# Reordering loads and statistics in a block of two half-step FFNs and a two-part mixer on eight cores

## The chip, the cores and the metric

One Trainium2 chip, eight cores, each working through two of the sixteen sequences. The two dies have cores 0 to 3 and 4 to 7. The metric is the device time of the slowest core, in microseconds. In slow executions a die's mean granted clock is lower; only fast ones are compared.

## The reference, cut

```python
D_MODEL, BATCH, SEQ, D_FF, EPS = 1024, 16, 2048, 2816, 1e-6

def rms_norm(x, g):
    y = x * lax.rsqrt(jnp.mean(x * x, axis=-1, keepdims=True) + EPS)
    return y * g

def swiglu(h, w_gate, w_up, w_down):
    return (jax.nn.silu(h @ w_gate) * (h @ w_up)) @ w_down

# one layer (cut):
x = x + 0.5 * swiglu(rms_norm(x, ffn1_norm), ffn1_w_gate, ffn1_w_up, ffn1_w_down)
h = rms_norm(x, mix_norm)
# ... h @ w_in gives q, k, v of a forgetting attention (8 heads x 64, causal, decay bias)
# ... and q, k, v, gates of a gated linear attention (4 heads, chunks of 64 frames)
x = x + concat(fox, gla) @ w_out
x = x + 0.5 * swiglu(rms_norm(x, ffn2_norm), ffn2_w_gate, ffn2_w_up, ffn2_w_down)
# and a final rms_norm
```

## The kernel before

A core has 4096 tokens, in eight groups of 512. The first FFN of groups 0 and 1 runs as a pair, so that the weights, which come as 32-bit numbers, are used twice in the stretch where the DMA engines are full (busy share 0.98 to 1.05 from 40 to 100 us, core 6); from then on a group's mixer runs interleaved with other groups' FFNs. The program is written as a list of operations with what they read and write. A scheduler in the program simulates the engines with estimated durations and so fixes the order on each engine; `level` is an operation's rank (0 is highest).

```python
        # DMA's end in the scheduler's simulation:
                dma_free = max(dma_free, t + o.dur) + o.nbytes / (o.rate * 1000.0)
                o.end = dma_free + 2000.0 + o.slack
```

A weight tile's first use loads it with a cast by the POOL queue and stores the bf16 copy; later uses load that copy by the SP queue. Some tiles are cast ahead in the background.

```python
        def LOADW(tag, wb, tile, src, keep, i, reads=()):
            # ...
            if key in uses:
                DMA("sp", (tag, wb, "b"), tile, keep[i], 2 * n, reads=[key], writes=[(tag, wb)])
                return
            uses.add(key)
            DMA("pool", (tag, wb), tile, src[i], 4 * n, reads=reads, writes=[(tag, wb)], slack=3000.0)
            DMA("sp", (tag, wb, "s"), keep[i], tile, 2 * n, reads=[(tag, wb)], writes=[key], level=1, slack=3000.0)
```

A norm's squares are summed over the 1024 channels with a matmul against ones; four small operations make the reciprocal root of it, and then the row of 512 values must be spread over the 128 partitions. There are two ways: eight small matmuls (0.61 us in the timeline of core 1) and an ACT copy (`spread`), or out to memory and back with a broadcast (`send`), which costs PE two such matmuls but takes two DMAs.

```python
        def rsqrt_columns(who, n, scale, bank, level):
            v, pw, hl = stat[who]
            TS(v[:, 0:n], banks[bank][:, 0:n], scale, EPS, ALU.mult, ALU.add, [], [PS(bank), ("stv", who)], level=level)
            P.op("pool", ...pow..., level=level)
            CP(hl[:, 0, 0:n], pw[:, 0:n], [("stp", who)], [("sth", who)], level=level)
            TT(hl[:, 1, 0:n], pw[:, 0:n], hl[:, 0, 0:n], ALU.subtract, [("stp", who)], [("sth", who)], level=level)

        def send_columns(who, n, out, otags, bank, level):
            # ... 2 matmuls and an ACT copy to stg
            DMA("sp", ("rw", who), rows_d[i, ...], stg[0:n, :], ..., writes=[("row", i)], level=level, slack=600.0)
            DMA("sp", ("rr", who), out, rows_d[i:i + 1, ...].broadcast_to([128, n * 128]), n * 65536,
                reads=[("row", i)], writes=otags, level=level, slack=800.0)
```

The start: x of group 0 on three queues, then weights, and the pair's first three tiles for each group.

```python
        for k in range(8):
            DMA(("sp", "act", "pool")[k % 3], ("x0", k), x_sb[:, 0, k, :], x_d[0, ...], 128 * 2048, writes=[("x", 0, k)], rate=0.35)
        DMA("sp", "gains", gT[:], gains_d[:, :], 16384, writes=["gT"])
        # ...
                todo = [(c, L) for c in range(NC2) for L in lanes]
                if pair and half == 0:
                    todo = [(c, L) for L in lanes for c in range(3)] + todo[6:]
```

The softmax here doesn't subtract the row's maximum and nothing guards it: scores larger than these inputs give would overflow.

Of the kernel before, what the change touches and what calls it, by code (L numbers as in the profile page):

```python
# [239 lines left out]
def build_nc():  # L240
# [17 lines left out]
    with contextlib.ExitStack() as st:  # L258
# [146 lines left out]
        for w in ("F", "M"):  # L405
# [3 lines left out]
                                               fill=1.0, base=0, channel_multiplier=1), [], ["ident", "setup"], dur=400)  # L409
        for k in range(8):  # L410
            DMA(("sp", "act", "pool")[k % 3], ("x0", k), x_sb[:, 0, k, :], x_d[0, k // 2, :, (k % 2) * T:(k % 2 + 1) * T], 128 * 2048,
                writes=[("x", 0, k)], rate=0.35)
        DMA("sp", "gains", gT[:], gains_d[:, :], 16384, writes=["gT"])
# [22 lines left out]
        DMA("sp", "c_fb", fb[:], fb_d[:, :], 32, writes=["fb"])  # L436
        DMA("sp", "c_gon", gon[:], gon_d[:, :], 512, writes=["gon"])
        TSS(gon[:], gon[:], 0.5, ALU.mult, [], ["gon"])
        DMA("pool", "c_wg2a", wg2a[96:113, :], wg2a_d[:, :], 17 * 1024, reads=["wg2a"], writes=["wg2a"])
        DMA("pool", "c_wmisc", wmisc[:].rearrange("p k c -> p (k c)"), wmisc_d[:, :], 163840, writes=["wmisc"])  # L440
# [8 lines left out]
        def LOADW(tag, wb, tile, src, keep, i, reads=()):  # L449
# [3 lines left out]
            if key in uses:  # L453
                DMA("sp", (tag, wb, "b"), tile, keep[i], 2 * n, reads=[key], writes=[(tag, wb)])
                return
# [4 lines left out]
        def background(gate):  # L460
            if tiles:
                src, keep, i = tiles.pop(0)
                uses.add((keep.tensor.name, i))
                DMA("pool", ("cast", len(tiles)), keep[i], src[i], 4 * 128 * keep.shape[2], reads=[gate],
                    writes=[(keep.tensor.name, i)], slack=6000.0)
# [5 lines left out]
        def rsqrt_columns(who, n, scale, bank, level):  # L471
            v, pw, hl = stat[who]
            TS(v[:, 0:n], banks[bank][:, 0:n], scale, EPS, ALU.mult, ALU.add, [], [PS(bank), ("stv", who)], level=level)
            P.op("pool", lambda e: e.tensor_tensor(out=pw[:, 0:n], in0=v[:, 0:n], in1=mhalf[:, 0:n], op=ALU.pow),  # L474
                 [("stv", who), "mhalf"], [("stp", who)], dur=390.0 + 141.0 * n, lat=250.0, level=level)
            CP(hl[:, 0, 0:n], pw[:, 0:n], [("stp", who)], [("sth", who)], level=level)
            TT(hl[:, 1, 0:n], pw[:, 0:n], hl[:, 0, 0:n], ALU.subtract, [("stp", who)], [("sth", who)], level=level)
# [19 lines left out]
        class Norm:  # L497
# [20 lines left out]
            def sums(self, bank):  # L518
# [6 lines left out]
                rsqrt_columns(self.who, 4, 1.0, bank, level)  # L525
# [39 lines left out]

        def norm_later(norm, then):
            def spread(gate):
                norm.send(nxt("fb", 3))
                then()
# [4 lines left out]
        class Raw:  # L574
# [7 lines left out]
            def emit(self):  # L582
                for k in range(8):
                    TS(self.h[:, k, :], x_sb[:, self.g, k, :], gT[:, k:k + 1], 1.0, ALU.mult, ALU.mult, [("x", self.g, k), "gT"],
                       [(self.tag, k)], level=0.1)
                    self.norm.add(k, 6 + self.g)
                self.norm.finish(6 + self.g)
                TT(self.square, self.rstd, self.rstd, ALU.mult, [self.rtag], [self.qtag], level=0.1)

        def ffn(f, lanes, middle, nextx=None, casts=(0, 0), second=None, ending=None, late=False):  # L590
            pair = len(lanes) == 2
            xtiles = (5, 7, 9, 10) if late else (3, 5, 7, 9)
            for half in range(2):
                todo = [(c, L) for c in range(NC2) for L in lanes]
                if pair and half == 0:
                    todo = [(c, L) for L in lanes for c in range(3)] + todo[6:]
                where = {}
                for n, (cl, L) in enumerate(todo):
                    if second is not None and half == 0 and n == 2:
                        second()  # L600
                    if cl not in where:
                        where[cl] = wb = nxt("wgu", 4)
                        LOADW("wgu", wb, wgu[:, wb, :], wgu_d[f], wgu_s[f], half * NC2 + cl,
                              [("x", 0, 5)] if cnt["wgu"] <= 3 else [("x", 1, 7)] if cnt["wgu"] == 4 else ())
                    wb = where[cl]
                    w4 = wgu[:, wb, :].rearrange("p (g k f) -> p g k f", g=2, k=8)
                    bg = nxt("fb", 3)
                    bu = nxt("fb", 3)
                    raw = L.raw if half == 0 and cl < 3 else None
                    h, hk = (L.h, L.hk) if raw is None else (raw.h, raw.hk)  # L610
                    for g, b in ((0, bg), (1, bu)):
                        for k0, k1 in ([(k, k + 1) for k in range(8)] if cnt["wgu"] == 1 and g == 0 else [(0, 4), (4, 8)]):
                            MM(banks[b][:], [(w4[:, g, k, :], h[:, k, :]) for k in range(k0, k1)],
                               [("wgu", wb)] + hk[k0:k1], [PS(b)], start=k0 == 0, stop=k1 == 8)
                    r = nxt("th", 2)
                    if raw is None:
                        ACTV([(thF[:, r, :], banks[bg][:], AF.Tanh, None, 0.5)], [], [PS(bg), ("th", r)], level=0)
                    else:
                        TT(thF[:, r, :], banks[bg][:], raw.rstd, ALU.mult, [raw.rtag], [PS(bg), ("th", r)], level=0)
                        ACTV([(thF[:, r, :], thF[:, r, :], AF.Tanh, None, 0.5)], [], [("th", r)], level=0)  # L620
                        TT(banks[bu][:], banks[bu][:], raw.square, ALU.mult, [raw.qtag], [PS(bu)], level=0)
# [14 lines left out]
                for d in range(8):  # L636
                    wb = nxt("wd", 4)
                    LOADW("wd", wb, wd[:, wb, :], wd_d[f], wd_s[f], half * 8 + d, [("x", 1, 7)] if cnt["wd"] <= 4 else ())
                    for L in lanes:
                        b = ring[n % 2]  # L640
                        n += 1
                        for c0, c1 in ((0, 5), (5, NC2 - 1), (NC2 - 1, NC2)):
# [4 lines left out]
                            [PS(b), ("x", L.xb, d)], level=0)  # L647
# [18 lines left out]
        def ffn1_pair(middle):  # L666
# [4 lines left out]
            def second():  # L671
                for k in range(0, 8, 2):
                    load_x(1, k, ("wgu", 0))
# [23 lines left out]
        def last_down(L):  # L697
# [6 lines left out]
            for d in range(8):  # L704
                if d < 4:
                    wb = nxt("wd", 4)
                    LOADW("wd", wb, wd[:, wb, :], wd_d[1], wd_s[1], 8 + d)
# [445 lines left out]
```

## Time and profile before

| | before |
|---|---|
| time, median of 4 runs | 2671.16 us (2667.99 to 2679.67) |
| spans of the eight cores in the profiled run | 2652.0 to 2667.5 us, mean 2660.2 |
| PE busy | 96% |
| last of the 96 matmuls of the start | 52.1 us |

The profile's views are read in this order: the busy shares, PE's waits by what ended them, PE's timeline where the waits lie. The prediction shows their lines.

### The profile page before, as it was taken

The page shows a single profiled execution, that of the slowest core. Times are in us where ns is not written, and L with a number is a line of the kernel's source. Part 1 is how long each engine was busy: PE and PEld are TensorE (multiplying, and loading weights), DVE is VectorE, ACT ScalarE, POOL GpSimd, SP SyncE. Part 2 cuts the span into 40 slices and gives each one's busy share as a digit, 9 for nine tenths or more (in the row PEclk, how much of TensorE's full clock was granted, in tenths as well). Part 3 has the DMA queues.
Part 4 walks back from the last instruction along what each step waited for, and adds up shares of the span by engine and source line. Part 5 has one row for each costly group of instructions (what it writes and reads, how often), then busy time and mean ns, then how long its engine had stood idle before and what let it go on. Part 6 is the DMA issues. An engine that isn't in the chain of part 4 may idle for free.

```text
span 2667.5 us, 42806 instructions; the slowest of 8 cores (2652.0 to 2667.5 us)
## 1 busy us (share of the span) xinstructions
PE 2559.5 (96%) x13691; PEld 1173.9 (44%) x13940; DVE 1724.2 (65%) x2807; ACT 951.5 (36%) x2070; POOL 766.1 (29%) x768
## 2 busy tenths in 40 slices
PE   6999998989999999999999999999999999999998
PEld 3444453533543344533445344543445434533444
DVE  6334477658577845678756864569645697678754
ACT  2112223235326513166431411335222364266413
POOL 2213014124234512145421321024410254055410
PEclk9999999989999999999999999999999999999999
DMA  9987787595563355544455454553644433434353
GB/s 206 208 166 175 172 204 156 149 192 153 161 222 123 125 178 165 164 135 140 134 160 167 138 186 151 158 179 111 203 156 143 147 119 114 148 112 146 110 166 122
DMA packets 129866, 417.71 MB, mean 157 GB/s; under 512 B 15311, under 2 KB 17680, under 8 KB 129424
## 3 DMA queue, kind: packets, MB, share of 16 engines
q1 hardware_dynamic: 108128, 340.94, 40.2%
q0 software_dynamic: 20544, 72.98, 14.5%
q8 instruction: 117, 1.92, 0.3%
q10 hardware_dynamic: 976, 1.05, 0.1%
q14 instruction: 101, 0.83, 0.1%
HBM read 404.49 MB, written 59.86 MB: 174 GB/s over the span
## 4 chain that ended last, share of the span: by engine, by line
PE 84%; DVE 5%; issue 4%; DMA 4%; POOL 1%; ACT 1%; DVEq 0%; SPq 0%; POOLq 0%; ACTq 0%
PE bank L335 84%; DVE hF L379 1%; DMA rstdM<-rows 1%; DVE Pt L376 1%; DVE x_sb L379 1%; DMA mixw_t<-mixw 1%; DMA wd<-wds 1%; DMA wgu<-wgu 1%; ACT Pt L364 1%; POOL rstdM L376 1%; DMA rows<-wg2at 0%; DVE ga L376 0%; POOL ga L376 0%; DMA mixws<-mixw_t 0%; DMA gT<-gains 0%
## 5 line engine op out<-in xcount | busy, mean ns | idle before, releaser
L335 PE MATMUL bank<-hF,wgu 128*128 128x512 bf16 x5088 | 1181.4, 381 | 25.8 <-DVE thF L379 5.5
L335 PEld LDWEIGHTS bank<-hF,wgu 128*128 128x128 bf16 x5232 | 489.4, 98 | 628.6 <-issue 91.0
L335 PE MATMUL bank<-act,wd 128*128 128x512 bf16 (+2 forms) x2581 | 583.6, 376 | 16.3 <-DMA wd<-wds 8.1
L364 ACT ACTIVATE thF<-bank 128x512 f32<-128x512 f32 x346 | 207.3, 599 | 927.2 <-PE bank L335 924.0
L364 ACT ACTIVATE Pt<-bank,biasT 128x256 bf16<-128x256 f32 (+1 forms) x1152 | 428.5, 477 | 132.6 <-PE bank L335 127.8
L379 DVE SCALAR_TENSOR_TENSOR thF<-thF,bank 128x512 f32<-128x512 f32 x352 | 240.2, 682 | 256.1 <-ACT thF L364 248.6
L335 PEld LDWEIGHTS bank<-act,wd 128*128 128x128 bf16 x2640 | 247.9, 98 | 319.9 <-issue 44.5
L376 POOL TENSOR_TENSOR ga<-ga,Pt 128x512 f32<-128x512 f32 (+3 forms) x256 | 286.3, 1118 | 210.6 <-ACT Pt L364 118.9
L379 DVE SCALAR_TENSOR_TENSOR x_sb<-bank,x_sb 128x512 f32<-128x512 f32 (+2 forms) x264 | 175.9, 667 | 176.7 <-PE bank L335 174.3
L376 DVE TENSOR_TENSOR act<-bank,thF 128x512 bf16<-128x512 f32 x330 | 225.8, 684 | 65.4 <-PE bank L335 59.2
L376 DVE TENSOR_TENSOR ga<-ga,Pt 128x512 f32<-128x512 f32 (+3 forms) x256 | 206.4, 806 | 46.3 <-ACT Pt L364 36.7
L364 ACT ACTIVATE sqF<-x_sb 128x512 bf16<-128x512 f32 (+2 forms) x184 | 110.3, 609 | 265.8 <-DVE x_sb L379 219.0
L335 PE MATMUL bank<-hM,mixw_t 128*128 128x512 bf16 x875 | 197.8, 379 | 3.0 <-DVE cc L379 1.6
L335 PE MATMUL bank<-mixw_t,hM 128*128 128x256 bf16 x1280 | 143.1, 274 | 3.1 <-DMA mixw_t<-mixw 3.1
L335 PEld LDWEIGHTS bank<-mixw_t,hM 128*128 128x128 bf16 x1280 | 125.7, 98 | 20.8 <-issue 3.3
L376 POOL TENSOR_TENSOR rstdM<-rstdM,sqF 128x512 f32<-128x512 f32 x84 | 104.5, 1244 | 96.9 <-ACT sqF L364 85.8
L335 PEld LDWEIGHTS bank<-hM,mixw_t 128*128 128x128 bf16 x896 | 85.6, 98 | 104.6 <-issue 5.9
L474 POOL TENSOR_TENSOR stpM<-stvM,mhalf 128x8 f32<-128x8 f32 (+1 forms) x26 | 36.7, 1412 | 284.3 <-DVE stvM L383 284.3
L335 PE MATMUL bank<-cc,mixw_t 128*128 128x512 bf16 x500 | 116.9, 385 | 1.0 <-DVE x_sb L376 0.3
L335 PE MATMUL bank<-QT,KT 64*128 64x512 bf16 (+3 forms) x640 | 86.7, 349 | 12.6 <-DVE Pt L376 8.2
L1009 DVE RECIPROCAL sqM<-sqM 128x128 f32<-128x128 f32 x96 | 90.7, 945 | 11.6 <-ACT sqM L364 10.1
L335 PE MATMUL bank<-Pt,V 128*64 128x512 bf16 (+3 forms) x640 | 89.3, 359 | 0.8 <-DVE Pt L376 0.7
(162 smaller groups left out, 1987.4 us busy)
## 6 DMA issues: line engine op xcount, KB each, us to landing
wgu<-wgus SPq DMA_DIRECT2D x294, 512.0 KB, 3.7
wd<-wds SPq DMA_DIRECT2D x210, 352.0 KB, 3.2
mixw_t<-mixws SPq DMA_DIRECT2D x112, 512.0 KB, 3.8
wgu<-wgu POOLq DMA_DIRECT2D x36, 512.0 KB, 9.6
wgus<-wgu SPq DMA_DIRECT2D x36, 512.0 KB, 9.2
x_sb<-x POOLq DMA_DIRECT2D x28, 512.0 KB, 6.2
y<-x_sb POOLq DMA_DIRECT2D x56, 256.0 KB, 3.3
wd<-wd POOLq DMA_DIRECT2D x26, 352.0 KB, 6.4
```

Source lines behind the costliest of these rows:

```text
L335: ins = e.matmul(out, lhsT=l, rhs=r, start=s0, stop=s1)
L364: ins = e.activation(out=out, in_=in_, func=func, **kw)
L376: return DVE(lambda e: e.tensor_tensor(out=out, in0=a, in1=b, op=op), free_n(out), reads, writes, rate, eng, level)
L379: return DVE(lambda e: e.scalar_tensor_tensor(out=out, in0=a, scalar=s, in1=b, op0=op0, op1=op1), free_n(out), reads, writes, level=level)
L474: P.op("pool", lambda e: e.tensor_tensor(out=pw[:, 0:n], in0=v[:, 0:n], in1=mhalf[:, 0:n], op=ALU.pow), [("stv", who), "mhalf"], [("stp", ...
L1009: P.op("dve", lambda e, a=rcp[:, qs], b=src: e.reciprocal(out=a, in_=b), [], sq2 + ([PS(OB)] if p == 3 else []), dur=860.0, lat=180.0)
```

## The change

Its intent is to take PE's few long waits away without touching the arithmetic. Its four parts and their cost carry the prediction's letters: (a) a start in which the first three weight tiles are loaded beside x, into the idle buffers of the mixer, with group 1's x next and all else waiting, and 64 dummy matmuls, to have PE's clock up when the first weights come (it was 0.50 after the wait at 431 us, core 6 of the kernel before); (b) loads of gate/up and down tiles held back until the stage before is half done; (c) one norm spread by matmuls instead of rows, and four background casts moved from an FFN to the mixer of group 1; (d) the statistics' small operations at the highest rank, and the last mixer's squares summed by PE alone; (e) is what the holding costs. The diff, cut to its core:

```diff
+        DMA("sp", "gains", gT[:], gains_d[:, :], 16384, writes=["gT"], rate=0.25)
         for k in range(8):
-            DMA(("sp", "act", "pool")[k % 3], ("x0", k), ...)
+            DMA(("sp", "act")[k % 2], ("x0", k), ..., rate=0.25)
+        for i, cuts in enumerate(((0, 512, 1024, 2048), (0, 1024, 2048), (0, 1024, 2048))):
+            for j, (c0, c1) in enumerate(zip(cuts, cuts[1:])):
+                DMA("pool", ("first", i, j), mixw[:, i, c0:c1], wgu_d[0][i][:, c0:c1], 512 * (c1 - c0),
+                    reads=[("x", 0, 4)] if i == 1 else [("first", 0, 2)] if i == 2 else [], ...)
+        MMS([(banks[7][:, 0:128], onesD[:], onesD[:], True, True) for _ in range(64)], ["onesD"], [PS(7)])
+        for k in range(8):
+            DMA("sp", ("x1", k), x_sb[:, 1, k, :], ..., reads=[("first", 1, 1)], writes=[("x", 1, k)], rate=0.25)
 # ... first_tiles(): the 96 matmuls, group 0 k by k in its first tile, group 1 k by k over all three
                         LOADW("wgu", wb, ..., half * NC2 + cl,
-                              [("x", 0, 5)] if cnt["wgu"] <= 3 else [("x", 1, 7)] if cnt["wgu"] == 4 else ())
+                              [("x", 1, min(2 * cnt["wgu"] + 1, 7))] if cnt["wgu"] <= 4 else [("down", 2 * cl)] if cl < 4
+                              else ())
-                    LOADW("wd", wb, ..., half * 8 + d, [("x", 1, 7)] if cnt["wd"] <= 4 else ())
+                    LOADW("wd", wb, ..., half * 8 + d, [(lanes[-1].atag, 2 * d + 2)] if d < 4 and (pair or (wd_s[f].tensor.name, half * 8 + d) in uses) else ())
         def norm_later(norm, then):
+            later[0] += 1
+            here = later[0] == 2
             def spread(gate):
-                norm.send(nxt("fb", 3))
+                (norm.spread if here else norm.send)(nxt("fb", 3))
-            ffn(1, ..., middle, nextx, (0, 7 if tg == 0 else 0), ...)
+            ffn(1, ..., middle, nextx, (0, 0), ...)
 # in mixer(tgg), after the first QT, KT, V tiles and after kdec:
+                if tgg == 1 and i == 0:
+                    background(("QT", 1), -1)
 # in rsqrt_columns, four times:
-            ..., level=level)
+            ..., level=0)
-            norm = Norm(xb, sqM, "sqM", rstdF2[:, tgg % 2], ("rstdF2", tgg % 2), None)
+            norm = Norm(xb, sqM, "sqM", rstdF2[:, tgg % 2], ("rstdF2", tgg % 2), None, tgg == NTG - 1)
```

## The prediction

> **What bounds the kernel now.** I read the page's totals first, then the list of what TensorE (PE) waited for, then PE's timeline in the few stretches where the waits lie, and last the timelines of VectorE (DVE) and of the DMA issues there. All lines are of core 6, the slowest.
>
> ```profile
> PE 2559.5 (96%) x13691; PEld 1173.9 (44%) x13940; DVE 1724.2 (65%) x2807; ACT 951.5 (36%) x2070; POOL 766.1 (29%) x768
> ...
> PE 84%; DVE 5%; issue 4%; DMA 4%; POOL 1%; ACT 1%; DVEq 0%; SPq 0%; POOLq 0%; ACTq 0%
> ```
>
> PE is busy 2559.5 of 2667.5 us, so 108 us of idle time is all that a change of order can take back, apart from matmuls that run at a lowered clock. The change removes no matmul of the model. The list of PE's waits says where the idle time sits:
>
> ```profile
> PE bank L335 <- ACT sqF L364: 14.4, 6, 8.3
> PE bank L335 <- DVE thF L379: 11.3, 7, 4.4
> PE bank L335 <- DVE Pt L376: 9.0, 17, 1.9
> PE bank L335 <- DMA wd<-wds: 8.1, 1, 8.1
> PE bank L335 <- issue: 6.7, 42, 0.2
> PE bank L335 <- DVE sthF L376: 5.4, 2, 2.9
> PE bank L335 <- DMA wgu<-wgus: 4.6, 1, 4.6
> ```
>
> (total us, times, longest.) The big ones are single events, not a steady leak: one wait of 8.1 us for a down-projection tile, one of 4.6 us for a gate/up tile, one of 8.3 us for the first squares. So I go by stage. PE's timeline of the start (start us, us, what, idle before):
>
> ```profile
> 8.32 0.35 PE L335 MATMUL bank<-onesD,sqF 128*128 128x1 bf16 x8 [8.32 <-ACT sqF L364]
> ...
> 18.69 6.73 PE L335 MATMUL bank<-hM,wgu 128*128 128x512 bf16 x23
> 27.62 4.44 PE L335 MATMUL bank<-hM,wgu 128*128 128x512 bf16 x12 [2.21 <-DVE thF L379]
> ...
> 45.23 0.90 PE L335 MATMUL bank<-cc,wgu 128*128 128x512 bf16 x2 [3.43 <-DVE thF L379]
> 46.35 5.91 PE L335 MATMUL bank<-cc,wgu 128*128 128x512 bf16 x21 [0.22 <-DVE thF L379]
> 52.10 1.89 PE L335 MATMUL bank<-hF,wgu 128*128 128x512 bf16 x8
> ```
>
> The first matmul of the FFN is at 18.69 us. The three first weight tiles for both token groups (96 matmuls) are done at 52.10. Eight such matmuls take 1.89 us at full clock, some 20.8 us for 96, so 31 us are lost before 52.1. Two later stretches:
>
> ```profile
> 439.47 4.42 PE L335 MATMUL bank<-act,wd 128*128 128x512 bf16 x10 [8.13 <-DMA wd<-wds]
> ```
>
> ```profile
> 552.58 3.57 PE L335 MATMUL bank<-hF,wgu 128*128 128x512 bf16 x8 [4.60 <-DMA wgu<-wgus]
> 560.53 3.57 PE L335 MATMUL bank<-hF,wgu 128*128 128x512 bf16 x8 [4.38 <-DVE thF L379]
> 565.97 0.28 PE L335 MATMUL bank<-gq,Sbf 128*128 128x64 bf16 x4 [1.87 <-DVE Sbf L376]
> 567.93 0.37 PE L335 MATMUL bank<-gq,Sbf 128*128 128x64 bf16 x4 [1.69 <-DVE Sbf L376]
> ```
>
> ```profile
> 557.72 2.08 DVE L379 SCALAR_TENSOR_TENSOR hM<-x_sb,gT,rstdM 128x512 bf16<-128x512 f32 x3 [12.64 <-DMA rstdM<-rows]
> ```
>
> DVE stood 12.64 us before a product that needs rstdM, which came by a DMA out to memory and back; the thF product that PE needed was behind it.
>
> [...]after each gap above eight 128x512 matmuls take 3.57 us instead of 1.89. A gap thus costs its length and about 1.7 us more. [...]a DMA share of 1.04 in 20 to 30 us with two queues active. So moving the x tiles from three queues to two costs nothing. [...]in the trace the second alone, issued at 536.52, landed at 557.62: 21 us, of which most is queueing behind weights.
>
> **The change, part by part.**
>
> (a) The start. Gains go first. The first three weight tiles load at once into the mixer's idle buffers beside x0, the second group's x follows, and everything else (four down tiles, their stores, the stores of these three tiles) waits. 64 dummy matmuls warm the array. The order of instructions shows the gate matmuls now taken k by k as x arrives, before the statistics. What must arrive is unchanged: x0 2.10 MB, three tiles of 1.05 MB read, x1 2.10 MB, 7.34 MB in all. In the old trace x0, issued from 1.06 us, was in at 11.7; the weights were issued only then and landed at 17.7, 21.9 and 26.2, 4.2 us each or 0.25 MB/us. x0 and tile 0 together (3.15 MB) are then in at about 1.1 + 2.5 + 12.6 = 16 us, tile 1 at 20, tile 2 and x1 (another 3.15 MB, side by side) at 33. Tile 2 lies near 28, and group 1 needs eight k steps of six matmuls, 8 x 1.3 = 10.4 us, after that. With a partly cold clock [...]I put the end of the 96 matmuls at 43 us, against 52.1: 9 us. Against it stands DVE: three evacuations of four DVE operations of 0.68 us (8.2 us), eight hF2 products of 0.74 (5.9) and those of the next tiles (4.1) crowd into about 14 us, perhaps 2 us lost. The eight scalings of x1 move to ACT and spare DVE 8 x 0.48 = 3.8 us. The next tile's small DMA wait at 58 and similar ones: 1 us. Sum: 8 us.
>
> (b) Loads held back. A gate/up tile 0 to 3 of a half now waits for down tile 0, 2, 4, 6 of the half before, and a stored down tile d below 4 for activation tile 2d+2. In the trace the down tile awaited at 431 was issued at 422.2, behind three gate/up tiles of 1.05 MB issued at 406 to 415 for a stage that starts much later, and needed 17 us to land. With those behind it the wait goes: 8.1 us of idle and 4.42 - 2.2 = 2.2 us of cold clock. I count 8 of the 10.3.
>
> (c) The norm at 530. The second of these norms is spread by eight small matmuls (0.6 us) and an ACT copy (0.6) instead of the two DMAs, and four background casts move from the second FFN of group 0 to the mixer of group 1, where DMA has room (it ran at 0.4 to 0.5 in 480 to 520 us on another core). The stretch 547 to 570 loses 4.6 + 4.4 + 1.9 + 1.7 us of idle and twice 1.7 of cold clock: 16 us. I count 14.
>
> (d) Small things. The statistics' operations get the highest rank: 26 of them, PE waits of 1.3 us at 463 and the like: 1 us. In the last mixer PE sums the squares directly, without the POOL additions of 1.24 us: of the 2.8 us waited for hF at 2536 I count 2 us with the clock.
>
> (e) Cost. [...]There are 28 half passes of one group. I allow 2 us in all.
>
> Sum: 8 + 8 + 14 + 1 + 2 - 2 = 31 us; 2671 - 31 = 2640 us.
>
> **The rivals.** First, transfers hidden no better: the start is bound by the 7.34 MB, and x and weights side by side delay x, so that group 0 begins as late as before. For it: the DMA engines are at 0.9 to 1.0 for the first 100 us. Against: they sit idle after 11.7 us until the weights stream, and five tiles that nobody needs yet run in between. It would give 2648. Second, the wait moves: the held loads become late in every FFN, 28 times 1 us, or the DMA backlog of the start comes back at 100 to 300 us, where PE now waits for nothing. Against: a half's down part lasts 8 x 11 matmuls, 19 us, and a 512 KB load has a median of 3.7 us to landing. It would give 2660 to 2670. Third, DVE binds the start, group 1's three tiles being evacuated at once: 2645. Fourth, all goes well, the 3 us wait for mixer weights at 316 goes too and the cores draw together (they spread from 2652.0 to 2667.5, mostly by these same DMA waits): 2625.
>
> **Range and chances.** The parts are fairly independent; (a) may be 0 to 14, (b) 0 to 11, (c) 6 to 17, (e) up to 15. I predict 2640, with 2625 to 2657 for 8 in 10. Faster by over 2% means below 2617.7, a gain of 53 us; that is half of all idle time and beyond what the named stretches hold, 0.05. Slower by over 2%: 0.005. Within 2%: 0.945.
>
> **What would show it.** In the new profile: (a) the 96 matmuls end at 41 to 46 us, with the chain of waits there on DMA and not on the statistics; (b) no wait for wd at 400 to 440; (c) no DVE wait for rstdM near 500 to 550, and PE's clock there at 1.00; (d) the last hF wait under 2 us; (e) PE's waits for wgu and wd elsewhere under 3 us in sum. I am wrong if the start ends at 50 or later, if new DMA waits over 5 us stand between 100 and 400 us or after 600, or if the moved casts make the mixer of group 1 wait.

What is marked as cut in it are rules and figures that were not read from this case's traces. The sum came to 8 + 8 + 14 + 1 + 2 - 2 = 31 us, so 2640. Two of its numbers stand as estimates: the end of the 96 matmuls at 43 us, as far as it counts on a lowered clock in the k steps and on 2.5 us before x streams (in the trace x0 took 10.6 us; its 2.10 MB at the 0.25 MB/us of the weights leave 2.2), and the 2 us of (e). "Cold clock" is a granted clock of 0.50 in the windows of core 6 at 439 to 444, 552 to 556 and 560 to 564 us; it is 1.00 at 120 to 140. The two queues with a share of 1.04 are q0 and q1, at 0.78 and 0.26. The 34 transfers that bring a row back took 3.6 to 21.1 us on core 6, 4.3 at the median, so most of the 21 us is delay; the weight loads and stores issued beside it took 13.9 to 18.2 us to land, but that they are its cause was tested only later, by `e4_norm_by_rows`.

## More of the kernel before

One more view matters later: the span and the mean granted clock by die.

```profile
die 0 (median of its cores): 2659.1 us, clock 0.993
die 1 (median of its cores): 2662.3 us, clock 0.992
```

Both dies have practically the full clock (0.993 and 0.992).

## The result and the profile after

The changed kernel took 2657.38 us (median of 10 runs, 2654.29 to 2661.43) against 2670.46 of the kernel before beside it (median of 15, two of them slow). Ratios here are the mean time of one kernel's fast runs over that of the other's of the same rounds, so not quite the ratio of these medians: 0.9949, 95% interval 0.9939 to 0.9959. The gain is 13 us where 31 were predicted, and the time lies 0.4 us outside the predicted range.

The profile after is of core 5, the slowest. The page's totals and the chain that ended last:

```profile
PE 2590.9 (97%) x14034; PEld 1180.1 (44%) x14034; DVE 1717.5 (65%) x2797; ACT 956.6 (36%) x2079; POOL 762.7 (29%) x759
...
PE 85%; DVE 6%; DMA 4%; issue 3%; ACT 1%; POOL 0%; SPq 0%; DVEq 0%; ACTq 0%; POOLq 0%
```

PE's busy time is not to be compared with the 2559.5 us of before: there 13691 matmuls stand beside 13940 weight loads, so some 250 records are missing, and here none. In the chain the share of what has no visible reason (issue) fell from 4% to 3% and that of DVE rose from 5% to 6%; DMA stayed at 4%. The view by die is the first thing that stands out:

```profile
die 0 (median of its cores): 2639.3 us, clock 0.994
die 1 (median of its cores): 2652.2 us, clock 0.986
```

Die 0 gained 19.8 us over its median before, die 1 only 10.1. In all ten fast runs the slowest core was on die 1, and the mean clock of that die was below that of die 0. What PE waited for (total us, times, longest):

```profile
PE bank L335 <- DVE hF L379: 4.7, 1, 4.7
PE bank L335 <- DMA mixw_t<-wgu: 4.7, 1, 4.7
...
PE bank L335 <- DMA mixw_t<-mixw: 3.8, 3, 3.1
...
PE bank L335 <- DMA wd<-wds: 2.1, 2, 1.4
```

The waits of 8.1 us for a down tile, of 4.6 us for a gate/up tile and the 14.4 us for squares are gone from the list. New ones are the first weight piece (4.7 us, in the first 13 us) and the mixer's weights; the wait for hF at the end grew from 2.8 to 4.7 us. PE's timeline of the start (start us, us, what, idle before):

```profile
1.41 5.48 PE L335 MATMUL bank<-onesD 128*128 128x128 bf16 x64 [1.41 <-POOL onesD L394]
...
12.25 1.01 PE L335 MATMUL bank<-hM,mixw_t 128*128 128x512 bf16 x2 [4.68 <-DMA mixw_t<-wgu]
...
22.59 8.84 PE L335 MATMUL bank<-hM,mixw_t 128*128 128x512 bf16 x33
...
45.31 10.99 PE L335 MATMUL bank<-hF,wgu 128*128 128x512 bf16 x43
```

The dummies were 0.107 us apart until 4.7 us, 0.056 after that and 0.066 from 5.9; they were over by 6.9. PE then waited 4.68 us for weights, and the first real pair of matmuls took 1.01 us at a granted clock of 0.50 (12 to 14 us; 0.51 from 14 to 22). The 96 matmuls were done by 45.3 (42.7 on core 1), against 52.1. Look at the third line: 33 matmuls took 8.84 us, 0.268 each, at a clock of 0.81 (22 to 31 us); the 27 at 444 us in the next view, at 1.00, took 0.222 each. The stretch of the old wait for the down tile:

```profile
444.24 6.00 PE L335 MATMUL bank<-act,wd 128*128 128x512 bf16 x27
...
458.83 1.89 PE L335 MATMUL bank<-hM,wmisct 128*40 128x512 bf16 x8 [0.73 <-DVE x_sb L376]
461.66 0.37 PE L335 MATMUL bank<-wg2at,pieces 17*128 17x256 bf16 x2 [0.94 <-DVE pieces L391]
462.84 0.24 PE L335 MATMUL bank<-onesD,sqF 128*128 128x1 bf16 x4 [0.81 <-DVE sqF L391]
464.04 0.24 PE L335 MATMUL bank<-onesD,sqF 128*128 128x1 bf16 x4 [0.96 <-DVE sqF L376]
464.48 5.30 PE L335 MATMUL bank<-cc,mixw_t 128*128 128x512 bf16 x16 [0.20 <-DMA mixw_t<-mixw]
```

The down tiles no longer wait. But at the start of the mixer of group 1 five waits of under 1 us stand in a row, and the 16 matmuls after them take 5.30 us, at a mean clock of 0.68; in the kernel before (core 1) the same 16 took 3.63, at 1.00:

```profile
468.37 3.63 PE L335 MATMUL bank<-cc,mixw_t 128*128 128x512 bf16 x16
```

Short waits for DVE stood before these there too: 0.30, 1.34, 0.36 and 1.48 us on that core.

**Where the time went, by stage.** I laid each core's matmuls out by the work done before them (each at its full-clock time, 0.216 us for 128x512, the median distance of two at 120 to 140 us of the kernel before, core 6, at clock 1.00; dummies count nothing), so that the loss at a given work is how late PE was. The table has the change of the loss against the profiled run of before, mean of the eight cores, in us; the columns are the stages in us of PE work done. In every trace two of the eight cores lack some 250 matmul records, which shifts their stages; without these two cores single cells change by up to 2 us and sums by up to 4. The cores' mean span in the profiled run of before, 2660.2 us, was some 2 us above that of its fast runs on chips 3, 6 and 9 (2657.5 to 2658.6), so totals read about 2 us too good.

| kernel | 0-60 start | 60-350 | 350-410 down tile | 410-450 mixer 1 begins | 450-550 norm | 550-1000 | 1000-1300 | 1300-2480 | 2480 to the end, last mixer | sum |
|---|---|---|---|---|---|---|---|---|---|---|
| changed, first runs | -6.0 | +0.4 | -7.7 | +3.5 | -11.0 | +2.2 | +2.1 | -1.0 | +2.4 | -15.0 |
| changed, chips 3, 6, 9 (mean) | -8.6 | -0.2 | -7.8 | +4.1 | -10.3 | -0.8 | +2.0 | -2.7 | +0.8 | -23.4 |
| no hold | -8.3 | +1.8 | 0.0 | -0.1 | -10.6 | +3.9 | +0.8 | -1.4 | -0.3 | -14.1 |
| casts back | -8.4 | -0.5 | -8.2 | +5.0 | -4.7 | +3.3 | +2.6 | -3.6 | +0.9 | -13.5 |
| second norm by rows | -8.6 | +0.3 | -7.8 | +4.7 | -8.9 | -0.6 | +2.1 | -3.1 | +0.8 | -21.0 |
| old rank | -8.7 | +2.5 | -7.3 | +4.4 | -10.1 | +5.0 | +2.7 | -0.9 | +3.7 | -8.8 |
| last sums by POOL | -8.5 | -0.1 | -8.1 | +4.6 | -10.1 | -1.4 | +2.1 | -2.8 | +1.9 | -22.2 |
| start alone | -8.2 | +2.8 | -0.3 | +0.1 | 0.0 | -0.9 | -0.4 | -0.4 | -0.1 | -7.3 |
| norm and casts alone | -0.7 | -1.0 | -1.2 | +0.2 | -10.3 | +2.3 | +0.1 | -1.7 | 0.0 | -12.4 |
| rank alone | +0.1 | -1.3 | -1.0 | +0.1 | -0.8 | +6.3 | +0.1 | -0.2 | -0.2 | +3.0 |
| longer hold | -9.0 | -0.7 | -8.4 | +4.8 | -2.5 | +1.7 | +2.5 | -2.8 | +0.9 | -13.4 |
| rows later | -8.8 | +0.5 | -8.1 | +4.3 | -10.3 | +1.9 | +3.8 | +1.5 | +0.8 | -14.5 |
| old rank, rows later | -8.0 | +1.8 | -7.6 | +4.2 | -11.8 | +1.2 | +4.0 | +4.3 | +3.5 | -8.4 |

Three theories came out of this first profile. A: the terms were right and a lowered clock on one die of this chip took the rest. B: holding loads back moved the waits (the +3.5 at 410 to 450 and the mixer's weights). C: the small parts, rank and last sums, did harm.

### The profile page after: what moved, and what is told of

Its sections match the earlier page's. It is cut to its first block, busy times and chain, and to the rows that moved or that the text cites. A ratio compares the mean times of both kernels' runs of the same rounds, so it can differ in the third digit from the quotient of the medians.

```text
span 2659.8 us, 43278 instructions; the slowest of 8 cores (2634.5 to 2659.8 us)
## 1 busy us (share of the span) xinstructions
PE 2590.9 (97%) x14034; PEld 1180.1 (44%) x14034; DVE 1717.5 (65%) x2797; ACT 956.6 (36%) x2079; POOL 762.7 (29%) x759
## 4 chain that ended last, share of the span: by engine, by line
PE 85%; DVE 6%; DMA 4%; issue 3%; ACT 1%; POOL 0%; SPq 0%; DVEq 0%; ACTq 0%; POOLq 0%
PE bank L335 85%; DMA mixw_t<-mixw 2%; DVE hF L379 1%; DVE x_sb L379 1%; DMA wd<-wds 1%; DVE sqM L1060 1%; DVE Pt L376 1%; ACT Pt L364 1%; DMA ga<-rows 1%; DMA rstdM<-rows 1%; DVE act L376 1%; DMA x_sb<-x 0%; DVE hM L379 0%; DVE ga L376 0%; DMA mixws<-mixw_t 0%
## 5 line engine op out<-in xcount | busy, mean ns | idle before, releaser
L335 PE MATMUL bank<-hF,wgu 128*128 128x512 bf16 x5232 | 1194.0, 381 | 8.5 <-DVE hF L379 4.7
L335 PE MATMUL bank<-act,wd 128*128 128x512 bf16 (+2 forms) x2640 | 592.0, 378 | 4.8 <-DVE x_sb L379 2.5
L335 PE MATMUL bank<-hM,mixw_t 128*128 128x512 bf16 x944 | 216.3, 385 | 7.1 <-DMA mixw_t<-wgu 4.7
L335 PE MATMUL bank<-cc,mixw_t 128*128 128x512 bf16 x560 | 134.7, 394 | 0.9 <-DVE cc L376 0.6
L379 DVE SCALAR_TENSOR_TENSOR hF<-x_sb,gT,rstdF 128x512 bf16<-128x512 f32 x120 | 89.1, 789 | 2.8 <-ACT rstdF L364 2.0
```

What stands on the lines that cost most here:

```text
L335: ins = e.matmul(out, lhsT=l, rhs=r, start=s0, stop=s1)
L379: return DVE(lambda e: e.scalar_tensor_tensor(out=out, in0=a, scalar=s, in1=b, op0=op0, op1=op1), free_n(out), reads, writes, level=level)
```

## The experiments

All kernels below gave correct results. Where a table says "fast", it gives how many of the runs were fast and their mean.

### Does the gain depend on the chip? (the change unedited, three more times)

No edit.

> The changed kernel itself, unedited, as the control of these runs: the four kernels of the first call ran on another chip than the changed kernel's first runs. Theory C (the lowered clock of 0.812 belongs to the chip of the first runs, not to the dummies): on a chip whose die 1 shows no 0.812 stretches in fast runs it takes 2645 to 2650, as the kernel without the dummies did, and the spans of the two dies are alike. Theory W (the dummies set it off): die 1 is again 10 us longer than die 0 at a clock under 0.990, and the time is 2655 to 2660. If this chip shows the stretches for the other kernels of this call too, theory C stands as well.

> The changed kernel unedited, as the yardstick for these three and a third reading of the change: ratio 0.990 to 0.993 on a chip with clocks of 0.994 to 0.996 on both dies; 0.994 to 0.996 on a chip where one die is at 0.985 to 0.992, with stretches at 13/16 of the clock.

> The changed kernel unedited, a fourth reading, side by side with the next. If the chip lowers the clock of pairs of cores to 13/16, as the one of the first runs did, the ratio is 0.994 to 0.996 and the slowest core is on the die concerned; on a chip that doesn't, 0.990 to 0.993.

| run | chip | fast runs of all | mean | before, mean | ratio (95%) |
|---|---|---|---|---|---|
| after_again | 6 | 4 of 6 | 2647.8 | 2670.6 | 0.9916 (0.9901 to 0.9931) |
| g0_after_third | 9 | 3 of 7 | 2648.4 | 2670.3 | 0.9923 (0.9903 to 0.9943) |
| h0_after_fourth | 3 | 4 of 4 | 2648.6 | 2672.2 | 0.9910 (0.9895 to 0.9925) |

The dies of the first of these:

```profile
die 0 (median of its cores): 2638.3 us, clock 0.995
die 1 (median of its cores): 2635.2 us, clock 0.994
```

and on its core 5, the stretch of the start that took 8.84 us before, from the timeline:

```profile
22.36 7.29 PE L335 MATMUL bank<-hM,mixw_t 128*128 128x512 bf16 x33
```

On three other chips the change gains 22 to 24 us, not 13. The clock records of the first runs show what was different: on die 1 stretches at a granted clock of 0.8125 (the 0.812 and the 13/16 of the expectations), mostly of 15.1 us, always on a pair of cores (4 and 5, or 6 and 7) at the same moment: cores 4 and 5 at 21 to 54 us, and at 75, 250, 653, 770 and 1889; cores 6 and 7 at 29, 52, 645, 741, 765 and 2605 (the last for over 36 us). The first of all is at 5 us on cores 4 and 5, while the dummies ran. By an estimate from that clock, a busy stretch of 15.1 us costs 15.1 x (1 - 0.8125) = 2.8 us. The profile before has one such stretch on two cores (1892 us); the fast profiled runs on chips 2, 3, 6 and 9 have none. In the profiled run PE's busy time inside such stretches, times 0.1875, is 19 to 21 us on each core of die 1. The ten runs also carry their own control, the undisturbed die: the slowest core of die 0 was on average 11.2 us (5.1 to 14.8) ahead of the slowest of die 1, and with die 0 alone the mean time would have been 2645.9 us; on chips 3, 6 and 9 the slowest cores of the two dies are within 1.5 us on average. Theory A holds for some 10 of the missing 18 us. Two things stay open: only one batch of runs fell on that chip, so chip and moment can't be told apart; and why the kernel before, run beside it, kept its time there.

### Is it the dummy matmuls?

`e1_no_warmup`, the changed kernel without them (run again as `h1_no_warmup_again` next to the unedited one), and `e2_warmup_alone`, the kernel before with them:

```diff
-        MMS([(banks[7][:, 0:128], onesD[:], onesD[:], True, True) for _ in range(64)], ["onesD"], [PS(7)])
```

> The changed kernel without the 64 dummy matmuls; every engine's order is otherwise the same. Theory W (the dummies set off the lowered clock of 0.812 on die 1, which then costs the slowest core its gain): the 0.812 stretch at 5 us is gone, those of cores 4 to 7 in the first 80 us become fewer or go, cores 4 to 7 reach the spans of die 0, and the time falls to 2645 to 2652. Rival L ([...]the lowered clock comes anyway, dummies or not): 0.812 stretches on die 1 stay at 20 to 80 us and later, and the time stays within 2655 to 2660. On either theory the start itself loses nothing, because the changed kernel's array stood idle for 1 to 4.7 us after the dummies and ran its next matmuls at half clock: the 96 first matmuls end within 1 us of 42.7 (die 0).

> The kernel before with only the 64 dummy matmuls added at its start; order otherwise the same. Theory W: 0.812 stretches appear on die 1 in the first 80 us, where the kernel before had none, and the time rises by 3 to 8 us over the kernel before. Rival L: no such stretches at the start[...]; time within 2 us of the kernel before.

> The changed kernel without the 64 dummy matmuls, again. On a chip that lowers the clock: if the dummies bring it on, this kernel has no such stretch in the first 60 us and a ratio of 0.990 to 0.993, where the kernel with them has 0.994 to 0.996; if they don't, both are alike. On a chip that doesn't lower it, both are within 3 us, as they were on another chip.

| run | chip | fast | mean | ratio to before (95%) |
|---|---|---|---|---|
| e1_no_warmup | 6 | 4 of 6 | 2646.2 | 0.9906 (0.9891 to 0.9922) |
| h1_no_warmup_again | 3 | 4 of 4 | 2648.3 | 0.9909 (0.9892 to 0.9925) |
| e2_warmup_alone | 6 | 3 of 6 | 2671.0 | 1.0002 (0.9986 to 1.0017) |

The dummies are inert: beside the unedited kernel, without them, the time is the same (0.9906 against 0.9916, 0.9909 against 0.9910). The timeline of the kernel without them, core 1, shows why:

```profile
9.45 1.01 PE L335 MATMUL bank<-hM,mixw_t 128*128 128x512 bf16 x2 [1.20 <-DMA mixw_t<-wgu]
```

The pair takes 1.01 us there too: with the dummies the granted clock was at 0.50 again when the weights came (12 to 14 us, core 5 of the first runs). Whether they bring on the stretches at 0.8125 on a chip inclined to them is open: none of the later fast runs showed any, with dummies or without.

### What does holding the loads bring, and what does it cost?

`e3_no_hold` keeps the hold in the first FFN only:

```diff
-                              [("x", 1, min(2 * cnt["wgu"] + 1, 7))] if cnt["wgu"] <= 4 else [("down", 2 * cl)] if cl < 4
-                              else ())
+                              [("x", 1, min(2 * cnt["wgu"] + 1, 7))] if cnt["wgu"] <= 4 else ())
-                    ... if d < 4 and (pair or (wd_s[f].tensor.name, half * 8 + d) in uses) else ())
+                    ... if d < 4 and pair else ())
 # ... and the last FFN's down tiles likewise
```

> The changed kernel with the loads held back only in the first half of the pair; later gate/up and down tiles load as soon as their buffer is free, as before. If step (b) is right, the wait for a down tile near 410 to 440 us comes back with 5 to 10 us. If the hold is also what costs 4 us between 700 and 1300 us of work (theory H: bunched loads slow the row transfers of the norms from some 6 to 7 us to 9 us), those transfers are back at 6 to 7 us and the stretch loses 4 us less, so that the time is 0 to 5 us above the changed kernel. Rival R (the new rank of the statistics costs there): the row transfers and the loss of 700 to 1300 stay as in the changed kernel, and the time is 5 to 10 us longer.

Measured: 2654.9 (5 fast of 7, chip 6), ratio 0.9941 (0.9929 to 0.9954), so 7 us more than the unedited kernel on that chip. The wait for the down tile is back (PE's timeline, core 1):

```profile
435.32 3.93 PE L335 MATMUL bank<-act,wd 128*128 128x512 bf16 x10 [6.71 <-DMA wd<-wds]
```

In the table the row "no hold" has 0.0 at 350 to 410, and also -0.1 at 410 to 450. So the +4.1 there is the price of the hold, as theory B says: part of what is saved is paid back 20 us later. Core 5 of the unedited kernel shows the payment:

```profile
451.67 0.24 PE L335 MATMUL bank<-onesD,sqF 128*128 128x1 bf16 x4 [0.97 <-DVE sqF L376]
453.63 6.29 PE L335 MATMUL bank<-cc,mixw_t 128*128 128x512 bf16 x16 [1.73 <-DMA mixw_t<-mixw]
```

The mixer's tile was issued at 436.07 on core 1 and took 14.4 us to land, with gate/up tiles that were held until then, their stores and down tiles beside it; in the kernel before, the same load took 8.8 us. And the granted clock was 0.5 there (for 3.4 or 6.8 us on seven cores; on core 1 from 446.8 us, in the third of waits of 0.73, 0.94 and 0.81 us; on core 5 of the first runs from 465.5 us). On core 1 the wait for the tile (2.28 us) and the slow 16 matmuls (5.10 us for 3.63) make up the whole price; the short waits for DVE sum to some 3.5 us there in both kernels. By stage, hold and payment net 3.7 us at 350 to 450; of the rest of the 7 us, 2.0 lie at 60 to 350 and 4.7 at 550 to 1000, where the order may be what differs (see below), less what other stages give back. What I had expected of the rows did not hold: without the hold the row transfers did get faster (median 7.3 us against 8.3), and yet 550 to 1000 lost more.

I took the tiles held there to be used only after 505 us, so holding them longer looked like a version that beats both. (In fact PE uses the first of them at 478.84 us on core 5.) `f3_hold_longer`:

```diff
-                              ... [("down", 2 * cl)] if cl < 4
+                              ... [("QT", 1) if f == 1 and half == 0 and lanes[0].xb == 0 and cnt["wd"] < 64 else ("down", 2 * cl)] if cl < 4
```

> The changed kernel with one more step of the same kind: the first four gate/up tiles of the second FFN of group 0, loaded at 413 to 448 though they are used only after 505, wait for the first queries of the mixer of group 1 (about 470). If the loss of 4.5 us left at 410 to 450 is the same backlog of transfers, the wait of 2.3 us for the mixer's weights at 448 goes and the time falls by 2 to 5 us: 2643 to 2647 on the chip where the changed kernel takes 2648.7, ratio about 0.990. If that loss is mostly the half clock after the short waits for DVE at 442 to 448, or if the tiles now collide with the moved casts, it stays within 2 us or grows: 2647 to 2655.

Measured: 2660.3 (4 fast of 6, chip 2), ratio 0.9964 (0.9946 to 0.9982): a miss, about 12 us worse than the unedited kernel on the other chips. PE's waits on core 5:

```profile
PE bank L335 <- DMA mixw_t<-mixws: 12.8, 3, 6.4
```

Four gate/up tiles with their stores now go at 470 to 507 us, on top of the moved casts, and the mixer's tiles beside them take 11 to 17 us where they took 4 to 8 in the changed kernel: the row "longer hold" loses 7.8 us against the changed kernel at 450 to 550. But the payment is gone from its old place. PE's timeline, core 5:

```profile
448.76 0.37 PE L335 MATMUL bank<-wg2at,pieces 17*128 17x256 bf16 x2 [0.94 <-DVE pieces L391]
449.07 1.90 PE L335 MATMUL bank<-cc,mixw_t 128*128 128x512 bf16 x8
450.81 0.24 PE L335 MATMUL bank<-onesD,sqF 128*128 128x1 bf16 x4
450.91 1.89 PE L335 MATMUL bank<-cc,mixw_t 128*128 128x512 bf16 x8
...
483.10 6.33 PE L335 MATMUL bank<-hM,mixw_t 128*128 128x512 bf16 x16 [4.75 <-DMA mixw_t<-mixws]
```

The 16 matmuls run at full clock with no wait before them. On all eight cores the mixer's tile landed in 7.3 to 8.5 us (12.1 to 14.4 in the unedited kernel), and no core's clock fell between 440 and 460 us. The loss from 410 to 440 us of work is 4.8 us here, 10.4 in the unedited kernel and 6.3 in the kernel before (the six cores with all records). The +4.8 of the table's column hides this: the new wait of 4.75 us at 478 falls before 450 us of work as well. So theory B is shown at this place: the price of the hold was the tile that came late behind the held loads. Holding them longer removes it, and charges more where those loads now go. A point between the two was not tried.

### What is the norm at 530 worth, and which half of it?

`e4_norm_by_rows` takes the rows again, with the casts in their new place; `e7_casts_back` has the casts in the FFN again and the norm spread; `f4_norm_alone` is the kernel before with just these two.

```diff
 e4:
-            here = later[0] == 2
+            here = False
 e7:
-            ffn(1, ..., middle, nextx, (0, 0), ...)
+            ffn(1, ..., middle, nextx, (0, 7 if tg == 0 else 0), ...)
-                if tgg == 1 and i == 0:
-                    background(("QT", 1), -1)
 # ... and the other three
```

> The changed kernel with the second norm sent by the two row transfers again, the four background casts staying in the mixer of group 1. Theory N (the transfer's queueing makes the stall, so either remedy would do): the transfer lands in under 10 us as DMA has room, VectorE waits for rstdM under 3 us, and the time is 0 to 2 us longer. Rival (the spread by matmuls is what removes it): the transfer still takes 15 us or more, VectorE waits 8 us or more, and PE loses 8 to 14 us near 520 to 550.

> The changed kernel with the four background casts back in the second FFN of group 0, the second norm still spread by matmuls. The run with the row transfers back lost only 1.5 us near 450 to 550 us of work, so the casts' place should be what counts. Theory N (DMA load makes that stall): PE loses 4 to 10 us more in that stretch than in the changed kernel, by a wait for weights. Rival (either remedy is enough): under 3 us more.

> The kernel before with the four casts moved to the mixer of group 1 and the second norm spread by matmuls; nothing else. By the prediction this is worth 14 us: 2657, ratio 0.995, and the DVE wait of 12 us for rstdM near 545 is gone. Putting the casts back into the changed kernel cost 10 us and putting the row transfers back cost nothing, so 10 us, 2661, is what I expect. If the parts only work together (the wait for the down tile at 431 stays, and the new order costs elsewhere), it is 2666 or more.

| run | chip | fast | mean | ratio to before (95%) |
|---|---|---|---|---|
| e4_norm_by_rows | 6 | 5 of 6 | 2647.6 | 0.9914 (0.9902 to 0.9926) |
| e7_casts_back | 6 | 4 of 5 | 2658.1 | 0.9953 (0.9939 to 0.9967) |
| f4_norm_alone | 2 | 4 of 6 | 2659.4 | 0.9961 (0.9947 to 0.9974) |

The place of the casts is the part that counts: with it alone (e4) the stage 450 to 550 gains 8.9 of 10.3 us, with the spread alone (e7) 4.7. With the casts away the two row transfers took 14.1 us together on core 5 (first issue to last landing), where they took 26.8 in the kernel before, and DVE's wait for the row (timeline, e4, core 5) is

```profile
530.45 2.74 DVE L379 SCALAR_TENSOR_TENSOR hM<-x_sb,gT,rstdM 128x512 bf16<-128x512 f32 x4 [3.22 <-DMA rstdM<-rows]
```

3.22 us, where the kernel before had 12.64 on its slowest core (and 4.25 on core 1). The spread of the second norm is then worth 1.4 us in its stage and nothing that the time shows. With the casts back, core 7 (PE's waits) has gate/up tiles late again:

```profile
PE bank L335 <- DMA wgu<-wgu: 4.1, 2, 2.4
...
PE bank L335 <- DMA wgu<-wgus: 1.6, 1, 1.6
```

Alone on the kernel before, the two gain 10.5 us, as expected; this is the only part whose worth is the same alone and in company.

### The rank and the last sums

`e5_old_rank` gives the statistics' operations their old rank, `f1_rank_alone` is the kernel before with the new rank, `e6_last_norm_pool` has POOL add the last mixer's squares again.

```diff
 e5:
-        def rsqrt_columns(who, n, scale, bank):
+        def rsqrt_columns(who, n, scale, bank, level):
-            ..., level=0)
+            ..., level=level)
 e6:
-            norm = Norm(..., None, tgg == NTG - 1)
+            norm = Norm(..., None, False)
```

> The changed kernel with the statistics' four operations at their old rank. Prediction of step (d): 1 us slower than the changed kernel. Rival R (the rank costs where it lets statistics overtake work that PE waits for): the loss near 410 to 450 us of work, 5 us more than in the kernel before, shrinks by 2 us or more, and the time is 1 to 4 us shorter than the changed kernel's. If neither, within 1 us.

> The kernel before with the statistics' operations at the highest rank, and nothing else. Taking the rank out of the changed kernel cost 12 to 20 us. If the rank has that worth by itself, this kernel needs some 2655 us (ratio 0.994), with shorter waits in the stages 250 to 350, 700 to 1000 and in the last mixer. If the rank has its worth only in company (the loss without it came from the new places of the casts and from the order that the scheduler then builds), this kernel is within 4 us of before: 2667 to 2675, ratio 0.9985 to 1.0015. My prediction of 1 us for it belongs to the second.

> The changed kernel with the last mixer's sums of squares taken by POOL again. The first wait for hF after it, 4.7 us in the changed kernel and 2.8 us before, should be back near 2.8 us if the direct sums lengthen it; the time then falls by 1 to 2 us. If the direct sums help, as step (d) had it, the wait grows over 4.7 us. Nothing else in the order moves.

| run | chip | fast | mean | ratio to before (95%) |
|---|---|---|---|---|
| e5_old_rank | 6 | 3 of 7 | 2668.5 (one of them 2680.2; the others 2661.3 and 2663.9) | 0.9992 (0.9962 to 1.0022) |
| f1_rank_alone | 2 | 4 of 7 | 2676.2 | 1.0024 (1.0010 to 1.0037) |
| e6_last_norm_pool | 6 | 4 of 6 | 2648.1 | 0.9919 (0.9904 to 0.9934) |

The last sums move nothing in the time (1.1 us in their stage). With POOL's sums the wait of 4.7 us for hF is gone, but four others of 1.0 to 2.0 us stand in its place (cores 1 and 5). The rank was the surprise: alone it costs 6 us, and taking it out costs 15 to 21 (without and with the run of 2680.2). Neither is 1 us, and they have opposite signs. In both cases much of the loss lies at 550 to 1000 us (+6.3 and +5.0 in the table), where kernels before and after lose least. DVE's and PE's timelines of the old-rank kernel there, core 7:

```profile
749.69 0.75 DVE L379 SCALAR_TENSOR_TENSOR lsg<-bank,gont,ga 128x512 bf16<-128x512 f32 x1 [3.82 <-DMA ga<-rows]
```

```profile
750.59 0.39 PE L335 MATMUL bank<-gq,Sbf 128*128 128x64 bf16 x8 [3.62 <-DVE lsg L379]
```

DVE was given a product that needs a row still under way; PE, whose order the program fixes, stood behind it with FFN matmuls next in its list. That led to a theory of order: the scheduler's formula lets the two row transfers be over some 7 us after the row is ready (I had put 6.5 in what I expected), the traces have a median of 7.1 us in the kernel before (272 rows) and 8.3 in the changed one (264), from the end of the ACT copy to the landing, so a new order may place a consumer too early. Two kernels test it; `g1_rows_later` changes one number in the changed kernel, `g2_old_rank_rows_later` the same in e5, and `g3_no_warmup_rows_later` the same in e1:

```diff
-                reads=[("row", i)], writes=otags, level=level, slack=800.0)
+                reads=[("row", i)], writes=otags, level=level, slack=2800.0)
```

> The changed kernel, with one number of the scheduler's model changed: the row transfer that brings a norm back is taken to land 2 us later, as the traces have it (8.7 us from the sum to the landing in the changed kernel, some 6.5 us in the model). Theory of order: what the rank and the other parts gain or lose after 550 us depends on whether DVE is given a product that needs the row before the row is there. Then the waits of DVE for rows (2 to 12 us in sum on a core) nearly vanish, and the time is 2644 to 2649 where the changed kernel has 2648.7: it has little of that loss left. Rival: order is chance, a new order loses anywhere, 2650 to 2660.

> The changed kernel with the old rank, which cost 12 to 20 us, and with the row transfers taken to land 2 us later by the scheduler. If the old rank lost by late rows (a wait of 3.75 us for lsg at 744 behind a row of 8 tokens' groups, and the like), most of the loss comes back without the rank: 2648 to 2653. If the rank itself is what the statistics need, it stays near 2661 to 2668.

> As the first of these, without the 64 dummy matmuls. They moved nothing on two kernels, so this is within 3 us of the first: it is the version that I expect to beat both kernels, 2643 to 2649. If the dummies were what lowers the clock of some cores in the first 60 us on the chip of the first runs, and these runs fall on such a chip, only the kernels with dummies show it.

| run | chip | fast | mean | ratio to before (95%) |
|---|---|---|---|---|
| g1_rows_later | 9 | 3 of 5 | 2653.5 | 0.9937 (0.9920 to 0.9953) |
| g2_old_rank_rows_later | 9 | 4 of 5 | 2662.4 | 0.9970 (0.9955 to 0.9985) |
| g3_no_warmup_rows_later | 9 | 0 of 7 | none | every run was slow |

The theory of rows fell. The waits of DVE for rows did shrink (29.7 us over the eight cores, against 65.8 in the unedited kernel on the same chip), and yet the new order is 5 us worse there (three fast runs of each; the slowest of one lies below the fastest of the other, though the intervals above overlap), and the old rank regained little or nothing (2662.4 against 2662.6 to 2668.5). So late rows are where the one loss of 3.6 us above came from, but not what makes an order good or bad. What is left is the rival that stood with it: each edit rebuilds the order on every engine, and a rebuilt order may lose somewhere. g1 changes no operation, one estimate alone, and a diff of PE's merged order (some 1490 rows on core 1) has over a thousand lines. Past 550 us and before the last mixer the changed kernel has -1.5 us in the table; of the eleven edited kernels in it, eight lose 2 to 11 us against that, spread over waits of around 1 us. I call this the chance of the order; it fits the runs, but only g1 tests it. That the rank has a fixed worth is not supported. One piece follows it, the last mixer: +3.7 with the old rank and the new last sums, +3.5 in g2, +0.8 with the new rank. Which edit makes which order lose, beyond the wait shown, stays open.

### The start by itself

`f2_start_alone`: the changed kernel with holds (but in the first FFN), casts, norm, rank and last sums undone; the diffs are those above, taken together.

> The changed kernel with everything but its start undone: loads not held (but for the first FFN), casts and second norm as before, old rank, last sums by POOL. If the start stands alone, its 96 matmuls end near 43 us and the time falls by the 8 to 11 us lost less there: 2660 to 2663 us, ratio 0.996 to 0.997. If the 9 us come back later, because the later stages are bound by transfers that were put off (four down tiles and stores of the start), the wait for the down tile at 431 grows and the time is 2667 to 2671.

Measured: 2665.6 (3 fast of 6, chip 2), ratio 0.9986 (0.9967 to 1.0004). The start itself gains the 8.2 us of its stage; 2.8 us are lost again at 60 to 350. In the whole change (-0.2 there) this loss does not appear. That the hold makes room for the transfers that the start put off would explain it, and the kernel without the hold does lose 1.8 there; but the kernels with the hold and the old rank lose as much (+2.5 and +1.8), so the cause is not shown.

No version beat the changed kernel beyond the intervals. Without the dummies it is as fast, with 64 matmuls fewer.

## Why the prediction was wrong

The sum was 31 us. On the three chips without the stretches at 0.8125 it is 22 to 24; on that of the first runs 13. So the clock took some 10 us; the rest of the miss is some 4 us each in (c) and (d) and 3 in (e), less small gains elsewhere. The ceiling of 108 us of idle time was itself too high: core 6's trace lacks 249 matmuls, and on core 5, with all of them, PE was idle for 92 of 2666.8 us. By its steps:

**(a) The start, 8 us: right.** 8.6 measured by stage. The 96 matmuls end at 42.1 to 45.3 us (the six cores with all records), inside the 41 to 46 named. The chain there lies on x's transfers until 15.4 us, though then for 3 us on the squares, which I had said it would not. The dummies, which were to have the clock up, gain nothing (it was 0.50 when the weights came); they had been given no number. The third rival, DVE binding the start, shows as waits of 1.55 and 1.9 us after 50 us (core 1), where 2 us had been allowed.

**(b) Loads held back, 8 us: right in size (7.8), and the wait is gone.**

**(c) The norm at 530, "I count 14": too big by 4.** The mechanism held (no DVE wait for rstdM at 500 to 550, and PE's clock at 1.00 there on cores 1 and 5), and alone the part gave the same 10.3. Nearly all of it is the casts' new place (8.9 in e4), not the spread. The 16 us had been read on core 6, the slowest of that profile, where this wait was among the longest; over the eight cores the kernel before lost some 12 us there on average (7.5 to 17.2). The wait differs from core to core, and the slowest cores were those where it was long (DVE stood 12.64 us for rstdM on core 6, 4.25 on core 1).

**(d) The small things, 3 us: wrong.** The last mixer's stage lost 0.8 us instead of gaining 2, and the wait for hF grew to 4.7 us where "under 2" was expected. (The direct sums alone are still 1.1 us better there than POOL's.) The rank was taken to be worth the waits that stand at its operations, 1 us; the runs give it no fixed worth: putting it in alone costs 6 us and taking it out costs 15 to 21, with the order rebuilt everywhere.

**(e) The cost, "I allow 2 us in all": too small by about 3.** 4.1 us at 410 to 450, which is not there without the hold, and about 1 of the 2.0 at 1000 to 1300. The cost did not come as a late load behind held ones in every FFN, as I had it, but once: among 32-bit weights and their stores, the next mixer tile came late (12 to 14 us to land, 7.3 to 8.5 when the held loads wait longer), and the granted clock was 0.5 at that place. My second rival had named "the wait moves" and sought it at 100 to 300 us.

**Not in the sum at all: the clock, the step that failed by most.** The sum lowers the clock only after waits of PE, and none of the rivals let the granted clock of a die fall in fast runs. That cost some 10 us on the chip of the first runs (11.2 between the slowest cores of the two dies of the same runs), and without it the time lies inside the range. With 22.9 us, the gain on chip 6, 2670.5 would have become 2648, 8 off the 2640.

## What to carry to other kernels

Read a wait's worth from all cores, not from the slowest, which is the slowest because its waits were long; and when a hold takes a wait away in a stage that is full of transfers, look for the bill in the next 20 us. In a kernel whose order comes from a scheduler, an edit of rank or of an estimate is a change of the whole order: test it alone and by taking it out, and believe only what agrees. Before explaining a gain that came out too small, compare the dies' clocks and run the unedited kernel on another chip.
